# The rests of the gates' weights: written negated by VectorE, completed by an accumulating DMA from GpSimd

## The chip, the cores and the metric

The kernel runs on one core of a Trainium2 chip. The metric is the device time of one execution in microseconds. The engines are TensorE (PE, with its weight loads PEld), VectorE (DVE), ScalarE (ACT), GpSimd (POOL) and SyncE (SP), which issues most loads; transfers run on 16 DMA engines.

## The reference

One layer of a hybrid decoder for a prompt of 512 tokens plus 16 meta tokens, and for 8 samples of 8 tokens with a paged past of 2048. All projections of the normalised input come out of one matrix `w_in`; this case is about its last two parts, the gates:

```python
xn = rmsnorm(x, p['ln_mix_pre'])
h = xn @ p['w_in']
da_q, da_k, da_v, gdn_qkv, gdn_z, gdn_b, gdn_a, gate_a, gate_b = jnp.split(h, SPLIT_POINTS, axis=-1)
...
mix = jax.nn.sigmoid(gate_a) * (o_a @ p['w_branch_a']) + jax.nn.sigmoid(gate_b) * (o_b @ p['w_branch_b'])
x = x + rmsnorm(mix @ p['w_out'], p['ln_mix_post'])
```

Everything is float32. `gate_a` and `gate_b` have 1024 channels each.

## The kernel before, in words

**Products in three parts.** The operands of a projection are of a rounded float32 type (`F32R`). To keep float32's accuracy each is split into a rounded part (hi) and a rest (lo = raw - hi), and a product is hi x hi + hi x lo + lo x hi. The input's parts `xhi` and `xlo` are kept for the whole first half. A weight tile of 1024 x 128 is split when it is needed: SP loads it in two halves of 256 KB (`wraw`, three buffers), ScalarE casts each to `whi` (one tile of eight blocks for both halves, two buffers), and VectorE subtracts the cast from the raw weights into `wlo` (one tile for each half, four buffers). `weight` does all this; `split` at lines 330 to 332 has the two instructions.

**A gate** (`gate`, numbered 0 to 15) is one such weight tile against 578 columns of the input, in two stretches of 256 and 322 columns. For each of the eight blocks of weights three products stand in a row, with hi, hi and lo as weights, so the first use of the rest is the third product of a gate. Then ScalarE takes tanh out of PSUM into `gt`. 48 products in all.

**Order of the work.** The gates are fillers. A planner (`merge`) interleaves two streams by planned shares of TensorE time: `main` holds the gated delta rule's chain (`gdn_chain`, one head after another, a long row of small dependent steps) and its projections, `rest` holds the samples' attention, then the 16 gates, then branch a. A scheduler then fixes the order of each engine's queue at build time, and each queue is worked off in that order. The gates stand between 460 and 604 us of the span, beside the chain of the heads 2 and 3 and, after 597 us, the first branch.

**Names that the prediction uses.** In `gdn_chain`, `hss` and `gf` and `grr` are small arrays that GpSimd raises to the power -0.5 (`rsqrt`, lines 398 to 401); `gf` scales the head's outputs `on` (line 1054), which TensorE then transposes. `out_new_gdn_prompt` and `out_new_gdn_sample` are the states' outputs, issued by GpSimd (lines 1048 and 1049). In `gdn_base` the rows `row` and `xc` (lines 1112 to 1114) are a Gaussian elimination of fourteen steps on VectorE, each a row operation of three instructions. `owhi` and `owlo` are the parts of `w_out`, loaded through the same three `wraw` buffers by `load_wout` while branch a runs; line 1654 multiplies a gate with its branch.

Of the kernel before, what the change touches and what calls it, by code (L numbers as in the profile page):

```python
# [9 lines left out]
F32 = mybir.dt.float32  # L10
F32R = mybir.dt.float32r
I32 = mybir.dt.int32
AF = mybir.ActivationFunctionType
ALU = mybir.AluOpType
# [138 lines left out]
WRAW, WLO = 3, 4  # L153
# [13 lines left out]
class Body:  # L167
# [172 lines left out]
    def split_w(self, raws, pool=None, eng=None):  # L340

        his, los = [], []
        pool = pool or self.wpool
        hi = self.t(pool, [128, 8, 128], "whi", F32R, bufs=2 if pool is self.wpool else 3)
        for j, raw in enumerate(raws):
            n = raw.shape[1]
            lo = self.t(pool, [128, 4, 128], "wlo", F32R, bufs=WLO if pool is self.wpool else 6)
            self.split(hi[:, 4 * j : 4 * j + n], lo[:, :n], raw, eng)
            his += [hi[:, 4 * j + i] for i in range(n)]
            los += [lo[:, i] for i in range(n)]  # L350
        return his, los

    def weight(self, src, c0, k0=0, nk=8, pool=None):
# [1276 lines left out]
    def gate(self, i):  # L1630
        m, j = divmod(i, 2)
        th = self.t(self.gtpool, [128, NQ], "gt", bufs=18)
        wt = self.weight(self.a["w_in"][0], self.GATES[j][0] + 128 * m)
        for half in HALF_Q:
            out = []
            yield from self.dense_steps(wt, self.x, half, out, 4)
            for p, c in out:
                self.nc.scalar.activation(th[:, c[0] : c[1]], p, AF.Tanh, scale=0.5)
            yield 0.0
        self.gates[i] = th  # L1640
# [763 lines left out]
```

## Time and profile before

| | |
|---|---|
| median of 3 runs | 1124.23 us (1124.17 to 1127.95) |
| profiled execution: span on the page, from its first to its last instruction | 1122.1 us |
| PE / PEld / DVE / ACT / POOL busy | 1100.6 / 972.3 / 731.3 / 524.7 / 224.9 us |
| rests of weights on VectorE (L332, `wlo<-wraw,whi`), whole kernel | 190 x 772 ns = 143.2 us |
| transfers issued by GpSimd (queue q0), whole kernel | 5.16 MB, 1.6% of the DMA engines' span |

The page gives the span of the profiled execution and no other time of it. Its busy shares are means over stages with different limits; the gates are one stage, and what they wait for is read from rows of that stage. A row of the timeline gives start, duration, engine, line, operation, output and inputs, and in brackets how long the engine had been idle and what ended that.

### The profile page before, as it was taken

What the parts mean: (1) busy time and instruction counts of PE and PEld (TensorE: products, weight loads), DVE (VectorE), ACT (ScalarE), POOL (GpSimd) and SP (SyncE); (2) the same over time, 40 slices, a digit from 0 to 9 for tenths busy, and PEclk for the clock granted to TensorE, in tenths of its full rate; (3) what the DMA queues carried; (4) which work ended last, traced back from release to release, by engine and by line L of the source; (5) the groups of instructions that cost most, each with busy time, mean ns of one, the idle gap of its engine ahead of it and who ended that gap; (6) DMA issues with size and microseconds to landing.
All of it is one profiled execution on the core that took longest, in us unless ns stands there. A gap on an engine that the chain in (4) does not pass through costs nothing.

```text
span 1122.1 us, 22894 instructions
## 1 busy us (share of the span) xinstructions
PE 1100.6 (98%) x8350; PEld 972.3 (87%) x8350; DVE 731.3 (65%) x1893; ACT 524.7 (47%) x1264; POOL 224.9 (20%) x336
## 2 busy tenths in 40 slices
PE   8999999999999999999999999999999999999997
PEld 7887797787787787799999987899999999988886
DVE  6456667695594477575344665599999999752315
ACT  6344444464464465452433244465555555832311
POOL 3231220210110110010000003344445454200000
PEclk9999999999999999999999999999999999999999
DMA  7385426847846856723234354323323332333213
GB/s 204 76 269 167 130 65 201 265 134 253 262 151 217 300 172 226 246 74 76 57 97 131 86 169 138 112 80 87 104 86 104 87 105 76 115 113 103 86 47 122
DMA packets 167354, 156.93 MB, mean 140 GB/s; under 512 B 12307, under 2 KB 123458, under 8 KB 167241
## 3 DMA queue, kind: packets, MB, share of 16 engines
q1 hardware_dynamic: 162833, 147.08, 42.8%
q0 software_dynamic: 3008, 5.16, 1.6%
q10 hardware_dynamic: 1400, 3.22, 0.9%
q8 instruction: 66, 1.08, 0.4%
q14 instruction: 47, 0.39, 0.1%
HBM read 145.54 MB, written 9.88 MB: 139 GB/s over the span
## 4 chain that ended last, share of the span: by engine, by line
PE 81%; DVE 8%; issue 3%; DMA 3%; ACT 2%; POOL 2%; SPq 0%; DVEq 0%; ACTq 0%; POOLq 0%
PE ps_d L289 30%; PE ps_t L289 22%; PE ps_g L289 16%; PE ps_s L289 6%; PE ps_t L437 6%; DVE cy L775 1%; DMA wraw<-in_w_out 1%; PE ps_m L289 1%; POOL grr L401 1%; DVE wlo L332 1%; DMA x<-in_x_prompt 1%; DVE row L1112 0%; ACT KT L1541 0%; DVE row L1113 0%; DVE xc L1114 0%
## 5 line engine op out<-in xcount | busy, mean ns | idle before, releaser
L289 PE MATMUL ps_d<-xhi,whi 128*128 128x256 f32 (+2 forms) x696 | 213.7, 310 | 0.1
L289 PE MATMUL ps_d<-xhi,wlo 128*128 128x256 f32 (+2 forms) x696 | 208.8, 303 | 1.5 <-DVE wlo L332 1.5
L332 DVE TENSOR_TENSOR wlo<-wraw,whi 128x512 fp32r<-128x512 f32 x190 | 143.2, 772 | 101.5 <-ACT whi L331 99.5
L289 PE MATMUL ps_d<-xlo,whi 128*128 128x256 f32 (+2 forms) x696 | 208.0, 302 | 0.0
L331 ACT CAST whi<-wraw 128x512 fp32r<-128x512 f32 x190 | 113.7, 621 | 167.2 <-PE ps_d L289 72.0
L289 PEld LDWEIGHTS ps_d<-xhi,whi 128*128 128x128 f32 x696 | 130.8, 189 | 5.9 <-issue 3.5
L289 PEld LDWEIGHTS ps_d<-xhi,wlo 128*128 128x128 f32 x696 | 130.5, 189 | 3.7 <-DVE wlo L332 2.0
L289 PEld LDWEIGHTS ps_d<-xlo,whi 128*128 128x128 f32 x696 | 131.1, 190 | 2.3 <-issue 2.0
L1541 ACT COPY KT<-ps_t 128x512 f32<-128x512 f32 x106 | 57.3, 601 | 34.3 <-PE ps_t L437 32.3
L332 DVE TENSOR_TENSOR lw<-sw,hw 128x512 fp32r<-128x512 f32 x76 | 69.8, 919 | 5.2 <-ACT hw L331 5.2
L437 PE MATMUL ps_t<-consts,page 128*128 128x128 f32 x512 | 68.1, 279 | 0.8 <-DMA page<-in_cache_k 0.6
L289 PE MATMUL ps_t<-fhit,hw 128*128 128x290 f32 x228 | 68.2, 299 | 0.1
L437 PEld LDWEIGHTS ps_t<-consts,page 128*128 128x128 f32 x512 | 55.6, 140 | 14.2 <-issue 7.8
L289 PE MATMUL ps_t<-fhit,lw 128*128 128x290 f32 x228 | 67.7, 297 | 0.0
L289 PE MATMUL ps_t<-flot,hw 128*128 128x290 f32 x228 | 67.7, 297 | 0.0
L331 ACT CAST hw<-sw 128x512 fp32r<-128x512 f32 x76 | 46.7, 617 | 18.3 <-PE ps_g L289 12.4
L289 PEld LDWEIGHTS ps_t<-fhit,hw 128*128 128x128 f32 x228 | 43.1, 189 | 0.3 <-DVE p L2069 0.3
L289 PEld LDWEIGHTS ps_t<-flot,hw 128*128 128x128 f32 x228 | 43.3, 190 | 0.0
L289 PEld LDWEIGHTS ps_t<-fhit,lw 128*128 128x128 f32 x228 | 43.2, 189 | 0.0
L2044 ACT ACTIVATE fy<-fpre,fw 128x592 f32<-128x592 f32 x22 | 19.5, 885 | 46.4 <-DVE fpre L2004 46.4
L2046 DVE SCALAR_TENSOR_TENSOR fy<-fpre,fw,fy 128x592 f32<-128x592 f32 x44 | 36.5, 830 | 1.0 <-ACT fy L2044 0.4
L289 PE MATMUL ps_s<-KT,qb 128*32 128x256 f32 x512 | 34.0, 385 | 0.6
(722 smaller groups left out, 2861.0 us busy)
## 6 DMA issues: line engine op xcount, KB each, us to landing
page<-in_cache_k SPq DMA_DIRECT2D x128, 256.0 KB, 4.2
page<-in_cache_v SPq DMA_DIRECT2D x128, 256.0 KB, 4.2
wraw<-in_w_in SPq DMA_DIRECT2D x86, 256.0 KB, 3.2
wraw<-in_w_ffn_in SPq DMA_DIRECT2D x50, 256.0 KB, 3.0
wraw<-in_w_down SPq DMA_DIRECT2D x44, 256.0 KB, 2.9
raw<-in_w_ffn_in SPq DMA_DIRECT2D x38, 256.0 KB, 3.0
wraw<-in_w_out SPq DMA_DIRECT2D x16, 256.0 KB, 3.1
x<-in_x_prompt SPq DMA_DIRECT2D x4, 512.0 KB, 7.0
```

The costliest lines, as they stand in the source:

```text
L289: return self.nc.tensor.matmul(out, lhsT, rhs, **kw).ins
L331: self.nc.scalar.copy(hi, raw)
L332: (eng or self.nc.vector).tensor_tensor(out=lo, in0=raw, in1=hi.bitcast(F32), op=ALU.subtract)
L401: nc.gpsimd.tensor_tensor(out=dst, in0=dst, in1=self.mhalf[:rows, :n], op=ALU.pow)
L437: self.nc.tensor.transpose(out, in_, self.ident[:k, :k])
L775: nc.vector.scalar_tensor_tensor(out=y, in0=pre[:, j : j + n], scalar=self.cw[:, ch, 24 + j : 25 + j], in1=y, op0=ALU.mult, op1=ALU.add)
L1541: copy(kt[:, :, 128 * j : 128 * j + 128], tp)
L2044: nc.scalar.activation(y, pre[:, 0:592], AF.Identity, bias=fw[:, m, 19:20], scale=fw[:, m, 16:17])
L2046: nc.vector.scalar_tensor_tensor(out=y, in0=pre[:, j : j + 592], scalar=fw[:, m, 16 + j : 17 + j], in1=y, op0=ALU.mult, op1=ALU.add)
```

## The change

The gates call a new `weight_dma` in place of `weight`. The load of the raw weights and ScalarE's cast stay. VectorE no longer subtracts: it writes the cast times -1 into `wlo`, from `whi` alone. Then a transfer issued by GpSimd reads the same 256 KB of raw weights from DRAM once more and adds them to what stands in `wlo`, which leaves raw - hi. There are 32 such transfers, 8 MB in all. The raw buffer `wraw` is now read by the cast alone.

```diff
+    def weight_dma(self, src, c0):
+        nc = self.nc
+        his, los = [], []
+        hi = self.t(self.wpool, [128, 8, 128], "whi", F32R, bufs=2)
+        for j, raw in enumerate(self.raw_w(src, c0)):
+            h = hi[:, 4 * j : 4 * j + 4]
+            lo = self.t(self.wpool, [128, 4, 128], "wlo", F32R, bufs=WLO)
+            nc.scalar.copy(h, raw)
+            nc.vector.tensor_scalar(lo, h.bitcast(F32), -1.0, None, op0=ALU.mult)
+            nc.gpsimd.dma_start(
+                lo, src[512 * j : 512 * j + 512, c0 : c0 + 128].rearrange("(k p) c -> p k c", p=128), accum_op=ALU.add
+            )
+            his += [hi[:, 4 * j + i] for i in range(4)]
+            los += [lo[:, i] for i in range(4)]
+        return his, los
 ...
     def gate(self, i):
         m, j = divmod(i, 2)
         th = self.t(self.gtpool, [128, NQ], "gt", bufs=18)
-        wt = self.weight(self.a["w_in"][0], self.GATES[j][0] + 128 * m)
+        wt = self.weight_dma(self.a["w_in"][0], self.GATES[j][0] + 128 * m)
```

The scheduler lays out the queues anew, and line numbers from 351 on are 16 higher in the changed kernel. Two places matter. The first is the end of head 2's chain, on GpSimd. Before, from the state's output of head 2 to that of head 3 (`gS` is the state, the number behind a name tells tiles of one kind apart):

```order
L1049 DMA out_new_gdn_sample<-st_5907 128x8x128
L401 TENSOR_TENSOR hss_6939<-hss_6939,mhalf_68 128x1
L1048 DMA out_new_gdn_prompt<-gS_7012 128x128
L401 TENSOR_TENSOR gf_7021<-gf_7021,mhalf_68 128x5
L401 TENSOR_TENSOR grr_7312<-grr_7312,mhalf_68 128x10
```

And now (`wlo_7193` and `wlo_7197` are the two halves of gate 1's rest, 7331 and 7335 of gate 2's, 7397 and 7401 of gate 3's):

```order
L1065 DMA out_new_gdn_sample<-st_5907 128x8x128
L362 DMA wlo_7193<-in_w_in 128x4x128
L417 TENSOR_TENSOR hss_6939<-hss_6939,mhalf_68 128x1
L362 DMA wlo_7197<-in_w_in 128x4x128
L1064 DMA out_new_gdn_prompt<-gS_7012 128x128
L362 DMA wlo_7331<-in_w_in 128x4x128
L417 TENSOR_TENSOR gf_7021<-gf_7021,mhalf_68 128x5
L362 DMA wlo_7335<-in_w_in 128x4x128
L362 DMA wlo_7397<-in_w_in 128x4x128
L362 DMA wlo_7401<-in_w_in 128x4x128
L417 TENSOR_TENSOR grr_7316<-grr_7316,mhalf_68 128x10
```

A transfer for a gate's rest now stands ahead of each of the three powers, two ahead of `grr`. The second place is the elimination of head 3 on VectorE, where the rest of gate 6 is made. Before:

```order
L1112 STREAM_SHUFFLE row_7480<-xc_7469 128x5x9
L332 TENSOR_TENSOR wlo_7674<-wraw_7669,whi_7673 128x512
L1113 TENSOR_TENSOR row_7480<-row_7480,lc_7467 128x5x9
L1114 TENSOR_TENSOR xc_7469<-xc_7469,row_7480 128x5x9
L332 TENSOR_TENSOR wlo_7677<-wraw_7671,whi_7673 128x512
L1112 STREAM_SHUFFLE row_7480<-xc_7469 128x5x10
```

And now:

```order
L1128 STREAM_SHUFFLE row_7488<-xc_7477 128x5x9
L1129 TENSOR_TENSOR row_7488<-row_7488,lc_7475 128x5x9
L1130 TENSOR_TENSOR xc_7477<-xc_7477,row_7488 128x5x9
L1128 STREAM_SHUFFLE row_7488<-xc_7477 128x5x10
L361 TENSOR_SCALAR wlo_7686<-whi_7681 128x512
L1129 TENSOR_TENSOR row_7488<-row_7488,lc_7475 128x5x10
L1130 TENSOR_TENSOR xc_7477<-xc_7477,row_7488 128x5x10
L1128 STREAM_SHUFFLE row_7488<-xc_7477 128x5x11
L361 TENSOR_SCALAR wlo_7690<-whi_7681 128x512
```

The first half's instruction stands one step of the elimination later, behind the shuffle of step 10 where it was behind that of step 9; the second half's moves by one and a bit. The other gates' instructions keep their neighbours on VectorE but for a place or two.

## The prediction
> **What bounds the kernel now.** I read the page's busy line first, then the row of the 100 us stretch in which most gates stand, then the waits of TensorE from the start of the gates to the end of the branches.
>
> ```profile
> PE 1100.6 (98%) x8350; PEld 972.3 (87%) x8350; DVE 731.3 (65%) x1893; ACT 524.7 (47%) x1264; POOL 224.9 (20%) x336
> ...
> 500.00:600.00 100.00, 100.00 (x782) 97.31 (x782) 47.95 (x136) 35.60 (x88) 2.70 (x3) 1.00 0.29 76
> ...
> PE ps_d L289 <- DVE gt L1654: 0.9, 1, 0.9
> PE ps_t L437 <- DVE on L1054: 0.5, 1, 0.5
> ```
>
> The second row lists, after the stretch and its length, the busy time of PE, PEld, DVE, ACT and POOL, then the granted clock, the DMA share and GB/s. TensorE has work all the time at the full clock; VectorE is idle for half of the stretch, GpSimd nearly always. The last two rows are all the waits of PE between 460 and 660 us: 1.4 us. So VectorE time taken away here is worth at most these 1.4 us, and the question is whether the new transfer makes TensorE wait.
>
> **Room for the transfer.** A gate's weights have two places, so the cast of one gate starts when the gate two before it has ended, and the gate in between is the time to get ready. The rows show this for gates 5, 6 and 7 in a row: the cast (ACT), the rest (DVE), and the first weight load of the rest (PEld).
>
> ```profile
> 503.44 0.62 ACT L331 CAST whi<-wraw 128x512 fp32r<-128x512 f32 x1 [0.96 <-PE ps_d L289]
> 504.49 0.68 DVE L332 TENSOR_TENSOR wlo<-wraw,whi 128x512 fp32r<-128x512 f32 x1
> 509.94 0.19 PEld L289 LDWEIGHTS ps_d<-xhi,wlo 128*128 128x128 f32 x1
> ...
> 509.87 0.62 ACT L331 CAST whi<-wraw 128x512 fp32r<-128x512 f32 x1 [3.02 <-PE ps_d L289]
> 511.37 0.68 DVE L332 TENSOR_TENSOR wlo<-wraw,whi 128x512 fp32r<-128x512 f32 x1
> 516.38 0.19 PEld L289 LDWEIGHTS ps_d<-xhi,wlo 128*128 128x128 f32 x1
> ...
> 516.30 0.62 ACT L331 CAST whi<-wraw 128x512 fp32r<-128x512 f32 x1 [3.02 <-DVE row L1112]
> 518.45 1.28 DVE L332 TENSOR_TENSOR wlo<-wraw,whi 128x512 fp32r<-128x512 f32 x2
> 522.81 0.19 PEld L289 LDWEIGHTS ps_d<-xhi,wlo 128*128 128x128 f32 x1
> ```
>
> Cast to cast is 6.43 us, the length of a gate with nothing else on PE. The same pair of rows, rest and first load of it, for the other gates with little room (1, 3, 10, 13, 15; of gate 10 the second half, whose first use is the fifth load of its rest), and last for gate 14, the least of all the others:
>
> ```profile
> 471.25 0.69 DVE L332 TENSOR_TENSOR wlo<-wraw,whi 128x512 fp32r<-128x512 f32 x1
> 477.82 0.19 PEld L289 LDWEIGHTS ps_d<-xhi,wlo 128*128 128x128 f32 x1
> ...
> 488.62 1.28 DVE L332 TENSOR_TENSOR wlo<-wraw,whi 128x512 fp32r<-128x512 f32 x2
> 494.46 0.19 PEld L289 LDWEIGHTS ps_d<-xhi,wlo 128*128 128x128 f32 x1
> ...
> 546.67 0.69 DVE L332 TENSOR_TENSOR wlo<-wraw,whi 128x512 fp32r<-128x512 f32 x1 [2.52 <-ACT whi L331]
> 553.15 0.19 PEld L289 LDWEIGHTS ps_d<-xhi,wlo 128*128 128x128 f32 x1
> ...
> 578.67 1.28 DVE L332 TENSOR_TENSOR wlo<-wraw,whi 128x512 fp32r<-128x512 f32 x2
> 584.12 0.19 PEld L289 LDWEIGHTS ps_d<-xhi,wlo 128*128 128x128 f32 x1
> ...
> 591.19 0.69 DVE L332 TENSOR_TENSOR wlo<-wraw,whi 128x512 fp32r<-128x512 f32 x1 [1.67 <-ACT whi L331]
> 597.00 0.19 PEld L289 LDWEIGHTS ps_d<-xhi,wlo 128*128 128x128 f32 x1
> ...
> 584.16 0.69 DVE L332 TENSOR_TENSOR wlo<-wraw,whi 128x512 fp32r<-128x512 f32 x1 [3.23 <-ACT whi L331]
> 590.56 0.19 PEld L289 LDWEIGHTS ps_d<-xhi,wlo 128*128 128x128 f32 x1
> ```
>
> **The change part by part.** Prices first: VectorE's one-source multiplications in SBUF, then GpSimd's transfers, with the time of the issue and the time from issue to landing.
>
> ```profile
> L1455 DVE TENSOR_SCALAR S<-S,rc 128x528 f32<-128x528 f32 x4 | 1.9, 486 | 0.0
> L1455 DVE TENSOR_SCALAR S<-S,rc 128x400 f32<-128x400 f32 x4 | 1.7, 424 | 0.1
> ...
> L1336 POOL DMA_DIRECT2D out_new_k_prompt<-kno x4: 802/825/988, 63.7 to 151.6; - x4
> DMA to landing us min/median/max: 1.6/3.4/7.3
> ...
> out_new_gdn_sample<-st POOLq DMA_DIRECT2D x4, 512.0 KB, 4.0
> out_new_k_prompt<-kno POOLq DMA_DIRECT2D x4, 256.0 KB, 3.7
> out_new_gdn_prompt<-gS POOLq DMA_DIRECT2D x4, 64.0 KB, 2.5
> ```
>
> *Negation for subtraction, 32 times.* Between the two multiplications, 128x512 costs 0.48 us (0.42 + 112/128 x 0.06) against 0.69: VectorE gives back 32 x 0.21 = 6.7 us, worth nothing on the path beyond the 1.4 us of waits. Bounds: 0.48, or 0.69 if the rounded output type keeps the slower rate.
>
> *The added transfer, 32 times, L us from issue to landing.* It is the one new link between VectorE and TensorE; no row shows an accumulating one. Lower bound 3.7 us, the plain 256 KB transfer of GpSimd, if the second operand's read costs nothing. Upper bound 2 x 3.7 = 7.4 us, as if a read and an add followed each other whole; the slowest landing of the k outputs, 7.3, lies there too. The nearest row is the 512 KB one, since an accumulation reads 256 KB of DRAM and 256 KB of SBUF: size costs (4.0 - 2.5) / 448 KB, 0.86 us for 256 KB more. I take 3.7 + 0.9 = 4.6 us.
>
> Room is from the negation's end (rest start + 0.48) to the first load: gate 1 6.1 us, gate 3 5.35, gate 5 4.95, gate 7 3.9, gate 10 6.0, gate 13 4.95, gate 15 5.3. Gate 7's negation ends about 0.8 sooner, since four rests ahead of it in VectorE's queue become 0.21 shorter: 4.7. Gate 6 would have 4.5, but its negation stands one step of the elimination later (0.7 us for a row operation of three), less 0.4 from two shorter ones: 4.2. Gate 14 has 5.9 us, and the wait of gate 13 ahead of it; the other gates have more. A gate that starts late gives the next one that much more room, since the next one's cast has started already. At L = 4.6 only gate 6 waits: 0.4 us. At L = 7.4 the waits are 1.3 (gate 1), 2.05 (3), 2.45 (5), 0.75 (6), 1.95 (7), 1.4 (10), 2.45 (13), 2.1 (15): 14.5 us. At 3.7 none.
>
> *Issues on GpSimd, 32 x 0.82 = 26 us.* That engine idles, so only what is queued behind matters. Three small operations of the chains now stand behind a transfer. Ahead of hss and grr the transfer's operand is there early. Ahead of gf it isn't:
>
> ```profile
> 478.10 0.60 POOL L1048 DMA_DIRECT2D out_new_gdn_prompt<-gS  x1 [4.21 <-DVE gS L1038]
> 478.91 1.19 POOL L401 TENSOR_TENSOR gf<-gf,mhalf 128x5 f32<-128x5 f32 x1 [0.20 <-DVE gf L400]
> 480.34 0.69 DVE L1054 TENSOR_TENSOR on<-on,gf 128x512 f32<-128x512 f32 x1
> 481.08 0.73 PE L437 MATMUL ps_t<-consts,on 128*128 128x128 f32 x5 [0.51 <-DVE on L1054]
> ```
>
> The state's output is issued at 478.10 to 478.70, then the new transfer to 479.5, and gf starts there instead of at 478.91: 0.6 us later, and with it on and TensorE's transposes, which wait already. Cost 0.6 us; between 0, if the transfer is issued while the output is still held up, and 1.4, if the issue takes twice as long.
>
> *Raw weights free after the cast alone.* Near the end of the gates the loads of the output weights wait for the last rest:
>
> ```profile
> 592.03 0.70 DVE wlo L332
> 592.75 3.13 DMA wraw<-in_w_out
> ```
>
> They can start at 592.0, the end of the cast, 0.7 us sooner; at the far end of that row of loads stands the wait of 0.9 us on gt. But gt itself has to follow its products, so I count 0 and keep 0.7 for the range.
>
> Sum: 0.4 + 0.6 - 0 = +1.0 us on a span of 1122.1. The median of the runs, 1124.23, lies 2.1 us above that span, taken as unchanged: 1125.2 us.
>
> On VectorE's rate the row of 486 ns for 528 columns shows the fast one. The Trainium skill (SBUF — State Buffer, Who interferes with whom) says that VectorE in its two-port mode, which one-source operations enter, holds the port pair that GpSimd needs to write descriptors, and that one blocks the other. The second negation of a gate would run within the first transfer's issue; by that rule, which no run here shows, L grows by up to 0.5, to an estimated 5.1, and the sum to +1.6 us (gates 5, 6 and 13 wait 1.0 in all), 1125.8. That is inside the case below and no rival of its own.
>
> **The rivals.** *The transfer is late.* If adding in flight is slower than a copy of twice the size, each gate with little room makes TensorE wait for its third product, and everything behind that in its queue. For it: nothing of the kind is in the profile, 256 KB out of one queue has taken 7.3 us, and a gate leaves only 4.2 to 6 us where loads of 2 x 256 KB run as well. Against it: the DMA engines are busy 29% of that stretch. It decides from L = 6.0, where the waits are 4.8 us and the sum 5.4 us. At 7.4 the time is 1124.2 + 14.5 + 0.6 = 1139.3 us; beyond, each us of L costs some 7 us more.
>
> *The waits of TensorE go.* If both waits vanish, because VectorE and the loads are ahead, and the transfer is hidden, the time is 1124.2 - 1.4 = 1122.8 us. For it: both waits end in VectorE. Against it: one is behind the delayed gf. It can't reach half a per cent.
>
> **How the numbers follow.** A change within 0.5% (5.6 us) is about what a measurement of this kernel can't tell from none. Transfer hidden or nearly so, L under 6.0: 0.58, with the waits gone as 0.08 of it. Transfer late: 0.38. Faster by more than the profile offers, by some change in the order that I don't see: 0.04. The time is that of the first, 1125.2; its own range is 1122.8 to 1129.8. The whole range has 1122.8 below, and above 1142, which is L = 7.7; I leave 0.15 beyond it, for an accumulation slower than both bounds.
>
> **What would show it.** Right: the rests' transfers land in about 4.6 us, the weight loads of the gates' rests have no wait but gate 6, the negations take 0.48 us, and the transposes of on start some 0.6 us later. Wrong: waits of TensorE or its weight loads for a transfer into wlo, at gates 3, 5, 7, 13 and 15 first, or casts more than 6.43 us apart where they were 6.43; or GpSimd's issues well over 0.82 us, so that grr and hss come late too.

## The result: half a per cent slower, and the profile after

The changed kernel takes 1131.36 us in the median of five runs, where the kernel before takes 1125.42 in the runs beside it. One of the five, the profiled one, ran at a mean granted clock of 0.554 and took 1770.48 us; it is left out of the ratio, 1.0046 (1.0026 to 1.0066), and every reading of the change below is from the profile of a repeat, the same kernel run again, at 0.997 and with a span of 1129.1 us. The repeat takes 1130.99 us (1130.88 to 1131.11) against 1125.58, a ratio of 1.0048 (1.0035 to 1.0062), 5.4 us (3.9 to 7.0).

First, of the repeat, the page's busy line, the row of the 100 us stretch that was shown of before, and all waits of TensorE between 460 and 660 us, where the kernel before had 0.5 us on `on` and 0.9 us on `gt`. The waits read: engine, tile and line, what released it, then the total in us, the number of times and the longest.

```profile
PE 1105.4 (98%) x8350; PEld 975.0 (86%) x8350; DVE 724.1 (64%) x1893; ACT 525.3 (47%) x1264; POOL 265.2 (23%) x368
...
500.00:600.00 100.00, 99.06 (x765) 95.06 (x764) 41.79 (x137) 34.20 (x86) 32.68 (x27) 1.00 0.79 130
...
PE ps_t L453 <- DVE on L1070: 1.8, 1, 1.8
PE ps_d L289 <- DMA wlo<-in_w_in: 0.9, 4, 0.4
PE ps_d L289 <- DVE gt L1670: 0.6, 1, 0.6
```

VectorE has lost 7.2 us of work and GpSimd gained 40. The share in which the DMA engines are busy went from 0.29 to 0.79 in that stretch, while the rate went from 76 to 130 GB/s. TensorE is no longer without a gap: a new wait for the transfers, and a wait on `on` more than three times as long. Two rows on the transfer itself: the issue's duration on GpSimd (minimum, median and maximum in ns), and the time from issue to landing.

```profile
L362 POOL DMA_DIRECT2D wlo<-in_w_in x32: 1264/1340/1853, 432.5 to 599.5; - x32
DMA to landing us min/median/max: 4.7/5.7/11.8
```

The issue takes 1.3 us where 0.82 was assumed, and the landing 5.7 us where 4.6 was. How late the repeat is, gate by gate, is told by the tanh of each gate's second half. First the kernel before, then the repeat: ends of gates 4, 5, 6, 7, 12, 13, 14 and 15.

```profile
510.40 0.43 ACT L1638 ACTIVATE gt<-ps_d 128x322 f32<-128x322 f32 x1
516.83 0.43 ACT L1638 ACTIVATE gt<-ps_d 128x322 f32<-128x322 f32 x1
523.26 0.43 ACT L1638 ACTIVATE gt<-ps_d 128x322 f32<-128x322 f32 x1
532.48 0.43 ACT L1638 ACTIVATE gt<-ps_d 128x322 f32<-128x322 f32 x1
...
577.60 0.44 ACT L1638 ACTIVATE gt<-ps_d 128x322 f32<-128x322 f32 x1
591.06 0.43 ACT L1638 ACTIVATE gt<-ps_d 128x322 f32<-128x322 f32 x1
597.49 0.43 ACT L1638 ACTIVATE gt<-ps_d 128x322 f32<-128x322 f32 x1
603.88 0.44 ACT L1638 ACTIVATE gt<-ps_d 128x322 f32<-128x322 f32 x1
```

```profile
514.38 0.43 ACT L1654 ACTIVATE gt<-ps_d 128x322 f32<-128x322 f32 x1
521.94 0.43 ACT L1654 ACTIVATE gt<-ps_d 128x322 f32<-128x322 f32 x1
529.07 0.43 ACT L1654 ACTIVATE gt<-ps_d 128x322 f32<-128x322 f32 x1
538.43 0.43 ACT L1654 ACTIVATE gt<-ps_d 128x322 f32<-128x322 f32 x1
...
583.53 0.44 ACT L1654 ACTIVATE gt<-ps_d 128x322 f32<-128x322 f32 x1
597.67 0.43 ACT L1654 ACTIVATE gt<-ps_d 128x322 f32<-128x322 f32 x1
604.10 0.43 ACT L1654 ACTIVATE gt<-ps_d 128x322 f32<-128x322 f32 x1
610.93 0.43 ACT L1654 ACTIVATE gt<-ps_d 128x322 f32<-128x322 f32 x1
```

The differences are 3.98, 5.11, 5.81, 5.95, then 5.93, 6.61, 6.61 and 7.05 us. So gate 5 loses 1.13 us, gate 6 0.70, gate 7 0.14, gate 13 0.68 and gate 15 0.44, 3.1 us in all, and the gates between 7 and 13 nothing. Of the 3.98 us ahead of gate 5, 1.7 are no effect of the change: the repeat's profile has them already at the state's output that the kernel before issues at 385.43 us and the repeat at 387.12, ahead of the first new transfer at 432.48. (The profiles differ so much by themselves: the kernel with six gates changed, told below, has that output at 388.15 and costs 0.3 us.) The other 2.3 us arise among gates 0 to 2; the longer wait on `on` is 1.3 of them, and the rest was not taken apart. Over the whole, the loss between 387 us and the end of the branches is 5.1 us.

Note how the two ways of counting differ. The list of waits gives 0.9 us for the rests on TensorE and 2.4 us on its weight loads, the tanh rows 3.1. Matmuls overlap in these records: where nothing waits, one of 256 columns starts every 0.12 us and has a duration of 0.28. So a gap shorter than the overlap shows as longer busy time and not as a wait. From the tanh of gate 3 to that of gate 15, TensorE's 778 matmuls are busy for 101.98 us of 102.99 in the repeat, and for all of the 99.92 us before.

### The profile page after: what moved, and what is told of

Its sections match the earlier page's. It is cut to its first block, busy times and chain, and to the rows that moved or that the text cites. A ratio compares the mean times of both kernels' runs of the same rounds, so it can differ in the third digit from the quotient of the medians.

```text
span 1768.7 us, 22953 instructions
## 1 busy us (share of the span) xinstructions
PE 1761.2 (100%) x8350; PEld 1393.5 (79%) x8350; DVE 707.5 (40%) x1893; ACT 542.7 (31%) x1264; POOL 242.2 (14%) x368
## 4 chain that ended last, share of the span: by engine, by line
PE 99%; DMA 0%; DVE 0%; ACT 0%; DVEq 0%; issue 0%; SPq 0%; ACTq 0%
PE ps_d L289 39%; PE ps_t L289 23%; PE ps_g L289 18%; PE ps_t L453 10%; PE ps_s L289 9%; PE ps_m L289 1%; DMA x<-in_x_prompt 0%; PE ps_s L453 0%; ACT junk L502 0%; PE lnb L453 0%; DVE yn L2325 0%; DVE xs L513 0%; DVEq L2416 0%; ACT yjunk L2297 0%; SPq L480 0%
## 5 line engine op out<-in xcount | busy, mean ns | idle before, releaser
L289 PE MATMUL ps_d<-xhi,whi 128*128 128x256 f32 (+2 forms) x696 | 291.3, 422 | 0.0
L289 PE MATMUL ps_d<-xhi,wlo 128*128 128x256 f32 (+2 forms) x696 | 287.5, 417 | 0.0
L289 PE MATMUL ps_d<-xlo,whi 128*128 128x256 f32 (+2 forms) x696 | 287.3, 417 | 0.0
L289 PEld LDWEIGHTS ps_d<-xhi,whi 128*128 128x128 f32 x696 | 173.8, 251 | 17.8 <-issue 6.9
L289 PEld LDWEIGHTS ps_d<-xlo,whi 128*128 128x128 f32 x696 | 174.7, 253 | 13.5 <-issue 3.5
L289 PEld LDWEIGHTS ps_d<-xhi,wlo 128*128 128x128 f32 x696 | 173.9, 252 | 13.5 <-issue 2.4
L332 DVE TENSOR_TENSOR wlo<-wraw,whi 128x512 fp32r<-128x512 f32 x158 | 105.4, 689 | 188.3 <-ACT whi L331 187.9
L453 PE MATMUL ps_t<-consts,page 128*128 128x128 f32 x512 | 107.2, 385 | 0.0
L362 POOL DMA_DIRECT2D wlo<-in_w_in x32 | 42.3, 1461 | 151.3 <-DVE wlo L361 66.8
L289 PE MATMUL ps_s<-page,pT 128*32 128x256 f32 x512 | 55.8, 577 | 0.0
```

The costliest lines, as they stand in the source:

```text
L289: return self.nc.tensor.matmul(out, lhsT, rhs, **kw).ins
L332: (eng or self.nc.vector).tensor_tensor(out=lo, in0=raw, in1=hi.bitcast(F32), op=ALU.subtract)
L362: nc.gpsimd.dma_start(lo, src[512 * j : 512 * j + 512, c0 : c0 + 128].rearrange("(k p) c -> p k c", p=128), accum_op=ALU.add)
L453: self.nc.tensor.transpose(out, in_, self.ident[:k, :k])
```

## The experiments

Eleven kernels ran, each timed against the kernel before on the same chip. The theories: *A*, the rest lands later than the gate's room and TensorE stalls; *B*, the issue on GpSimd is dearer than assumed and holds up the small powers behind it, gf first; *C*, the new order of the instructions itself.

**The change once more, without the transfer, and with a plain transfer.** The first is the changed kernel unchanged.

> The changed kernel once more, for a profile at the full clock and a second comparison. Theory A (the rests land later than the gates' room, TensorE stalls): 5 to 6 us over the kernel before, weight loads of the rests waiting 4 us or more in all, at gates 5, 6, 13, 3 and 7 first, and a landing of 5.5 to 6 us. Theory B (GpSimd's issues are dearer than 0.82 us, and the small powers queued behind them come late): the same time, but TensorE's waits are then on on, qk and the row products and not on wlo; an issue takes 1.4 us or more. Theory C (the new order of the instructions itself): waits on neither, and longer stretches of other work.

The second leaves out the transfer:

```diff
             nc.vector.tensor_scalar(lo, h.bitcast(F32), -1.0, None, op0=ALU.mult)
-            nc.gpsimd.dma_start(lo, src[...]..., accum_op=ALU.add)
```

> The changed kernel without the added transfer: the rest is only the negated rounded part (the raw weights are not added). The order of the other instructions is that of the changed kernel in all but a few rows. Theories A and B: within 1 us of the kernel before, 0 to 1.4 us under it, since neither the transfer nor its issue is there. Theory C: it stays 4 to 6 us slower.

The third keeps it as a copy:

```diff
-            nc.gpsimd.dma_start(lo, src[...]..., accum_op=ALU.add)
+            nc.gpsimd.dma_start(lo, src[...]...)
```

> The same 32 transfers from GpSimd, into the same places and behind the same negations, but plain copies that overwrite the negation (the rest is then the raw weight itself, nothing is added). It tells the addition from the transfer. Theory A: landing 3.7 to 4.6 us, so only gate 6 waits, and the time is within 1.5 us of the kernel before. Theory B: the issue costs the same (32 issues in the same queue), so most of the 5 us stays.

Measured: the repeat 5.4 us over the kernel before, as told above; without the transfer 1.0003 (0.9994 to 1.0012), 0.3 us; as a plain copy 1.0018 (1.0009 to 1.0027), 2.0 us. The waits of TensorE from 460 to 660 us without the transfer are these:

```profile
PE ps_t L450 <- DVE on L1067: 0.9, 1, 0.9
PE ps_t L450 <- DVE oS L1499: 0.2, 1, 0.2
```

The wait of 0.9 us on `gt` is gone, the one on `on` has grown by 0.4 through the new order, and one of 0.2 on `oS` is new. So theory C falls, and what VectorE gives back is worth nothing even when the transfer is free. The plain copy's rows show what the addition costs:

```profile
L362 POOL DMA_DIRECT2D wlo<-in_w_in x32: 740/748/914, 432.8 to 598.4; - x32
DMA to landing us min/median/max: 3.4/4.7/10.7
```

Each issue is 0.6 us shorter and the landing 1.0 us sooner. In the packet records of the two traces a packet of 512 bytes takes 65 ns with the addition and 42 without (medians). A transfer that runs alone, the first of gate 10, moves from 552.06 to 554.60 us with it and from 551.26 to 552.81 without. Two of a gate in a row take about 4.4 us with the addition, so the second one waits for the first. By the repeat, both A and B hold in part: issue and landing are about as A and B have them, but the weight loads wait for rests 2.4 us and not the 4 that A gave, and TensorE waits for `on` besides. The copy comes between them: a landing of 4.7 us and 2.0 us of time are a little over A's 4.6 and 1.5, and far from B's "most of the 5". Its issue is cheaper too, so this run does not part A from B. Its stalls are at gates 6 and 7 alone, and the usual landing explains neither. Part of the one at gate 7 has another cause (last section). At gate 6 the issue itself is late, as the first half's negation, the two issues and the first load of the rest show:

```profile
515.04 0.42 DVE L361 TENSOR_SCALAR wlo<-whi 128x512 fp32r<-128x512 f32 x1
517.23 1.49 POOL L362 DMA_DIRECT2D wlo<-in_w_in  x2 [6.75 <-DVE row L1128]
520.71 0.19 PEld L289 LDWEIGHTS ps_d<-xhi,wlo 128*128 128x128 f32 x1 [0.82 <-DMA wlo<-in_w_in]
```

The issue starts 1.77 us after the negation's end, and the transfer lands 3.4 us later, one of the two quickest. In the repeat the same issue starts 1.04 us after the negation. VectorE works on the elimination in both stretches; what holds the issue no row tells.

**Which gates cost.** Only the gates with long room take the transfer, then only gates 3 to 15, then three sets that together make the sixteen. Each is one line:

```diff
-        wt = self.weight_dma(self.a["w_in"][0], self.GATES[j][0] + 128 * m)
+        w = self.weight_dma if i in (0, 2, 4, 8, 9, 11, 12, 14) else self.weight
+        wt = w(self.a["w_in"][0], self.GATES[j][0] + 128 * m)
```

and with `i >= 3`, `(0, 1, 2)`, `(4, 8, 9, 11, 12, 14)` and `(3, 5, 6, 7, 10, 13, 15)` in its place.

> Only the gates with long room (0, 2, 4, 8, 9, 11, 12, 14) take the accumulating transfer, the other eight subtract as before. Theory A: no stall up to a landing of 5.9 us, so within 1 us of the kernel before. Theory B: half of the issues remain, among them the ones ahead of gf if these belong to gates 0, 2 or 4: 2 to 3 us slower.

> The change for gates 3 to 15 alone: gates 0 to 2, whose issues stand around the power gf, subtract as before. If the issues ahead of gf cost 1.2 us (theory B for this part), 3.5 to 4.5 us over the kernel before, the transposes of on wait 0.5 to 1 us, and the gates' stalls stay (5, 6, 13 and 15). If they cost nothing, 5 to 6 us as with all gates.

> The change for gates 0 to 2 alone, the complement of the run with gates 3 to 15. If the issues ahead of gf are the price there, 1 to 2 us over the kernel before, and on waits 1 to 1.5 us longer; no wait of gates 3 to 15.

> The change for gates 4, 8, 9, 11, 12 and 14 alone: over 5.9 us of room each, none of them beside gf. Theory A (only a landing later than the room costs, and the issues cost only where a chain's small power stands behind them): within 1 us of the kernel before. If each transfer costs something wherever it stands (12 of 32 here), 2 us over it.

> The change for gates 3, 5, 6, 7, 10, 13 and 15 alone, those with 3.9 to 6 us of room. Theory A: by a landing of 5.7 us 2.5 to 4 us over the kernel before, in waits of the rests' weight loads at gates 5, 6, 7, 13 and 15, up to 1 us more than in the run with all gates at gates 6 and 7, since nothing ahead of them moves their casts.

| gates with the transfer | ratio, 95% | us over before, by the ratio |
|---|---|---|
| 0 to 2 | 1.0019 (1.0010 to 1.0028) | 2.1 |
| 4, 8, 9, 11, 12, 14 | 1.0003 (0.9994 to 1.0012) | 0.3 |
| 3, 5, 6, 7, 10, 13, 15 | 1.0030 (1.0018 to 1.0041) | 3.4 |
| 3 to 15 | 1.0033 (1.0021 to 1.0045) | 3.7 |
| 0, 2, 4, 8, 9, 11, 12, 14 | 1.0038 (1.0026 to 1.0049) | 4.3 |
| all | 1.0048 (1.0035 to 1.0062) | 5.4 |

The first three sets add up to 5.8 us, the whole is 5.4. Three of the five sets came out as expected; gates 0 to 2 are just over, 2.1 us for 1 to 2, and the long-room set is a miss. Twelve transfers with room and with no chain behind them cost nothing that can be measured. The waits of TensorE, 460 to 660 us, first with the transfer at gates 0 to 2, then at the seven with little room:

```profile
PE ps_t L453 <- DVE on L1070: 1.9, 1, 1.9
PE ps_d L289 <- DVE gt L1671: 0.3, 1, 0.3
```

```profile
PE ps_d L289 <- DMA wlo<-in_w_in: 2.3, 5, 0.8
PE ps_t L453 <- DVE on L1070: 0.5, 1, 0.5
```

They part cleanly: the wait on `on` belongs to gates 0 to 2, the wait for the rests to the seven. The mechanism of the first stands in GpSimd's own rows; with the transfer at gates 3 to 15 alone, then at gates 0 to 2 alone:

```profile
479.53 0.60 POOL L1064 DMA_DIRECT2D out_new_gdn_prompt<-gS  x1 [4.23 <-DVE gS L1054]
480.33 1.19 POOL L417 TENSOR_TENSOR gf<-gf,mhalf 128x5 f32<-128x5 f32 x1 [0.20 <-DVE gf L416]
```

```profile
479.09 0.61 POOL L1064 DMA_DIRECT2D out_new_gdn_prompt<-gS  x1 [2.82 <-DVE gS L1054]
479.83 1.28 POOL L362 DMA_DIRECT2D wlo<-in_w_in  x1
480.61 1.72 POOL L417 TENSOR_TENSOR gf<-gf,mhalf 128x5 f32<-128x5 f32 x1
```

From the start of the state's output, gf is done after 1.99 us without the issue between them and after 3.24 with it: 1.25 us, and the wait on `on` is 1.4 longer.

The long-room set costs 4.3 us where theory A gave under 1. About half of it is one wait, at gate 2; the rest was not taken apart (the wait on `on` is 1.0 us there, 0.5 longer than before). In PEld's rows:

```profile
493.36 0.19 PEld L289 LDWEIGHTS ps_d<-xhi,wlo 128*128 128x128 f32 x1 [2.15 <-DMA wlo<-in_w_in]
```

With gates 1 and 3 subtracting, the second negation of gate 2 starts only at 486.13 us, and its transfer is held back besides (last section). In the kernel with all gates, gate 2 has no such wait: room is a property of one order of the instructions, not of the gate.

**More room for the rest.** The gates' products are put in another order: first all 32 products of the rounded weights, for both halves of the columns, then the 16 of the rests, so that the rest is first loaded some 4 us later, two thirds of the gate's 6.43 us.

```diff
-        for half in HALF_Q:
-            out = []
-            yield from self.dense_steps(wt, self.x, half, out, 4)
...
+        for half in HALF_Q:
...
+            for k in range(8):
+                self.mm(p, hi[k], xhi[:, k], start=k == 0, stop=False)
+                self.mm(p, hi[k], xlo[:, k], start=False, stop=False)
...
+        for p, xhi, c in ps:
+            for k in range(8):
+                self.mm(p, lo[k], xhi[:, k], start=False, stop=k == 7)
```

> The changed kernel with the gates' products in another order: the 16 products of the rounded weights for both halves of the columns first, then the rests' products of both halves. The first load of a rest then comes about 3 to 4 us later in its gate, so that a landing of 5.7 us fits in every gate's room. Theory A (stalls of the gates' rests make some 3 of the 5.4 us): 1.5 to 3 us over the kernel before, no wait of TensorE for a transfer into wlo. Rival (the gates' stalls are only where the loss shows, its source is the chain delayed by the issues): 4 to 6 us over it.

> The kernel before with that order of the gates' products alone, as the control of the run ahead of it: within 1.5 us of the kernel before by each theory; what it differs by is the price of the order and is to be taken off the run ahead.

> Both at once: gates 3 to 15 with the transfer, and the rests' products last in each gate. If stalls (3.1 us) and gf (1.2 us) are the whole, it is within 1 us of the control with that order of products. If 2 us or more stay, something else costs, such as the raw loads beside 13 x 2 more transfers.

| order of products, gates with the transfer | median us | ratio to before, 95% |
|---|---|---|
| rests last, none (control) | 1127.95 | 1.0024 (1.0015 to 1.0032) |
| rests last, all | 1129.36 | 1.0033 (1.0021 to 1.0045) |
| rests last, 3 to 15 | 1127.49 | 1.0017 (1.0008 to 1.0026) |

The control costs 2.7 us and so misses its 1.5; TensorE waits 0.9 us for a cast there, and the rest of it is not explained. So the run with all gates misses its 1.5 to 3 us over the kernel before too, with 3.7. Against the control, by the ratios, the change costs 1.0 us with all gates and -0.8 us with gates 3 to 15 (by the medians 1.4 and -0.5), where in the old order it costs 5.4 and 3.7. The landing is the same, and nobody waits for it; the rows of the run with all gates:

```profile
DMA to landing us min/median/max: 4.7/5.7/11.8
...
PE ps_t L453 <- DVE on L1070: 1.3, 1, 1.3
PE ps_d L289 <- ACT whi L331: 0.9, 2, 0.6
PE ps_t L453 <- DVE oS L1502: 0.3, 1, 0.3
PE ps_d L289 <- DVE wlo L332: 0.2, 1, 0.2
```

So the loss has two parts, each taken away by itself. The gates' stalls are 3.4 us by the run of the seven, 3.7 by gates 3 to 15, and 4.4 and 4.5 by what the later rests take away with all gates and with gates 3 to 15. The issues at gates 0 to 2 are 2.1 us alone, 1.7 as the difference between all gates and gates 3 to 15, and 1.0 as what stays with the rests last. The intervals of these, about 1 us each way and more for differences, don't part them finer. No version beats the kernel before. None is to be expected: with no transfer at all the change gains nothing.

## Why the prediction was right in kind and short in size

The forecast 1125.2 was about 6 us low; the measured time lies in its range of 1122.8 to 1142.0, at the edge of "within 0.5%", and above the likeliest case's own range, 1129.8.

- *VectorE's time is worth nothing on the path.* Right. The negation takes 0.43 us in the median, less than the 0.48 taken, and the kernel that has only this gain is at 1.0003. Of the waits of 1.4 us that it could have taken, the 0.9 on `gt` went there, and 0.4 at `on` and 0.2 at `oS` came in its place.
- *The landing L, 4.6 us.* This term was mis-sized, and it is the larger part of the error: 5.7 us measured. The working had 3.7 for a plain transfer and 0.9 for the addition. The runs have 4.7 for the plain transfer at this place and 1.0 more with the addition. So the addition was priced about right as a whole, though part of it is a longer issue, which the working did not have, and the base was 1.0 too low. It came from rows of the k outputs, which go from SBUF to DRAM between 64 and 152 us; here the transfers load from DRAM, mostly two in a row, beside the raw weights' loads. The one that runs alone, the first of gate 10, lands in 3.4 us as a copy and 4.8 with the addition, which points at the company and not at the direction; no run tests it.
- *The table from L to stalls.* Right in kind; that its sum fits is partly luck. Put at L = 5.7, the rooms given there yield about 0.4 us at gate 3, 0.75 each at gates 5, 6 and 13, 0.25 at gate 7 and 0.4 at gate 15, 3.3 us. Measured were 0 at gate 3, 1.13 at gate 5, 0.70 at 6, 0.68 at 13, 0.14 at 7 and 0.44 at 15, 3.1 us. That a stalled gate gives the next one room is to be seen at gate 14, which loses nothing. But 5.7 is the median of both halves of all gates, and the table weighs first halves alone (of gate 10 the second). The first halves of gates 5, 6, 7, 13 and 15 landed 4.9, 4.7, 5.9, 4.9 and 5.4 us after their issues; by the table gates 5 and 13 would then not wait. Two things that the working left out stand in the place of the difference. The room is counted from the negation's end, and these five issues start 0.3 to 1.0 us after it. And the second half can stall a gate once more, as at gate 5 in the repeat (first load of the rest, and fifth):

```profile
514.36 0.19 PEld L289 LDWEIGHTS ps_d<-xhi,wlo 128*128 128x128 f32 x1 [0.36 <-DMA wlo<-in_w_in]
516.50 0.19 PEld L289 LDWEIGHTS ps_d<-xhi,wlo 128*128 128x128 f32 x1 [0.65 <-DMA wlo<-in_w_in]
```

By the starts of TensorE's matmuls about half of the 3.1 us, 1.5, is lost at second halves.

- *The issue ahead of gf, 0.6 us.* The mechanism and the place are right, the size is not. It needed an issue of 0.82 us and had one of 1.3, since an accumulating issue is 0.6 us longer than a plain one (1340 to 748 ns). gf is done 3.23 us after the start of the state's output where it was 2.00, and the wait on `on` is 1.3 us longer, near the bound of 1.4 given for "the issue takes twice as long"; up to 0.4 of that wait is the new order.
- *The issues ahead of hss and grr: 0.* Right for TensorE. grr is not held up (1.87 us of waiting for it on VectorE, 1.85 before), though three issues stand ahead of it, not two. hss is: VectorE waits 1.63 us for it where it was 0.48, but no wait of TensorE in that run is put down to it.
- *Raw buffers free sooner: 0.* No run tested it by itself.
- *The rival "the transfer is late"* was to decide from L = 6.0, where the sum is 5.4 us. The same 5.4 came about at L = 5.7. There the table's 3.3 and gf's 1.3 make 4.6, and some 0.8 us have no term; the profile has them among gates 0 to 2. The result lies where the two cases meet.

On the rule weighed there, the Trainium skill (SBUF — State Buffer, Who interferes with whom) would have a negation on VectorE, in its two-port mode, hold up GpSimd's issue; the trace does not agree to any extent that counts. Rows of GpSimd in the repeat, the first with one issue alone and the second with both issues of gate 7, the first of which has the gate's second negation (522.91 to 523.34 us) beside it:

```profile
550.11 1.26 POOL L362 DMA_DIRECT2D wlo<-in_w_in  x1 [7.81 <-DVE grhs L990]
522.79 2.63 POOL L362 DMA_DIRECT2D wlo<-in_w_in  x2 [3.18 <-DVE wlo L361]
```

Half of 2.63 is 1.31 us, 0.05 over the lone issue, where blocking through a negation of 0.43 us would add that much. In the kernel with plain copies an issue with a whole negation beside it takes 0.84 to 0.91 us and a lone one 0.74, so 0.1 to 0.17 more. By these rows a negation lengthened L by little; the late issue at gate 6, told above, comes ahead of the issue and so is no part of L. The Trainium skill (Collectives: The Full Stack, The bandwidth ceiling: the fold count and why AG ≠ RS ≠ AR) says of sums between cores that an add in flight is slow because it reads two sources, and puts it at half the rate. The trace agrees in the direction: 65 ns a packet against 42, or 2.54 us a transfer against 1.55, which is 1.5 to 1.6 times and not twice.

## What to carry to other kernels

Before work is moved from an idle-enough engine to a transfer, measure the room between the operand's last write and its first use, gate by gate, and compare it with the landing of a transfer of the same kind, issued in the same burst; a copy's landing is too low a price for an accumulating one. Count the time from the last write to the issue too, and every part that lands by itself. Look also at what stands behind the issue on the issuing engine, since one issue ahead of a short operation of the chain cost about 1 us of the 5 here. And ask first what the freed engine's time is worth: leaving the new work out altogether answers that in one run.

## What was not expected of the hardware

A transfer lands only after its last packets, and in two places of these traces the last packets stand behind a packet of instruction code. In the kernel with plain copies the weights' load at gate 7 waited:

```profile
528.46 0.19 PEld L289 LDWEIGHTS ps_d<-xhi,wlo 128*128 128x128 f32 x1 [1.25 <-DMA wlo<-in_w_in]
```

The DMA view of the same kernel from 526.0 to 528.5 us shows what ran then. First the busy share in 40 slices, in tenths, and then the packets of each queue (number, MB, share of 16 engines):

```profile
DMA  9236100000000000000014111123111112112110
...
q0 software_dynamic: 58, 0.03, 12.1%
q8 instruction: 1, 0.02, 3.0%
q14 instruction: 1, 0.01, 1.4%
```

By the packet records, all but 35 of the gate's 1056 packets are done by 526.33 us. One packet of 16 KB of instructions runs from 526.04 to 527.25, and the 35 follow from 527.23 to 528.50, the rhythm of a single engine. At gate 2 of the kernel with the long-room set it is the same: a 16 KB packet from 491.07 to 492.03, then the last 13 packets from 492.02 to 492.71, where the others were done by 491.62. That makes about 1 us each time. That the two share an engine is read from these times; the records don't name the engine, and no run tried it by itself.
